# Sums of the MLP input's blocks kept in DRAM, and a second phase whose first operands are made in the first

## The chip, the cores and the metric

One core of one Trainium2 chip. The metric is the device time of one execution in microseconds; the output must agree with the reference.

## The reference, cut to what matters

One layer, 2048 tokens of width 1024, attention with a forget gate, then an MLP of width 4096. The change is in the MLP:

```python
x = x + g_m * fox_mixer(h, ...)                      # attention and its output projection
h = rms_norm(x, norm_mlp) * (1 + sc_f) + sh_f
x = x + g_f * (jnp.square(jax.nn.relu(h @ w_mlp_in)) @ w_mlp_out)
```

All of it is float32.

## The kernel before, in words

A float32 operand is held as two float32r parts: `split` makes the first by a cast on ACT (L754) and the second, the rest, by a subtraction on VectorE, DVE (L755). One product is then three matmuls (`mm3`, L139 to L141), first by first, first by rest, rest by first.

The two MLP products use a block scheme with seven products for eight (the Strassen-Winograd form). Operands are cut two by two, and products are named P1 to P7: P1 and P2 take blocks as they are, P6, P7, P5 and P4 take sums, P3 a sum on one side. The tokens are done in two halves s = 0, 1, each of two blocks of 512.

*Attention and output projection* come first; the projection works through 16 blocks of 128 tokens (`out_project`, 48 matmuls each). Beside it, from a list `side` of generators that are run one step at a time, the normed input h of the MLP is transposed (`turn`) and stored in DRAM as `h2_d`, for the first eight blocks; after the last of these, `prep_x(0)` loads the blocks B00 and B10 of h and splits them.

*Phase one* (h times W1, then relu and square) is a list of 224 slots, 112 for each half, one product of 12 matmuls in each. Jobs of kind X hold P1 and P2, jobs of kind Y hold P6, P7, P5, P4 and P3; each half begins with four X jobs, so that the first Y job is its ninth slot, and ends with four Y jobs. `prepare`, three slots ahead, blends the blocks of W1 on GpSimd (POOL, L966) and splits them. On the side, in a list `aux`, one generator step per slot: `prep_t(s)` loads four blocks of h for each of four kk, blends them on POOL into T1 to T4 (L807 to L814, 16 instructions a half) and splits five operands; then eight `turn_later` scale and transpose the tokens 1024 to 2047; then `prep_x(1)`, and after the last slot of the first half `prep_t(1)`. `mix` blends the results (four POOL instructions per Y job) for phase two, and `late` holds their stores to DRAM (`a_d`, `s_d`; L1058, for the last ones L1077), all on SP's queue.

*Phase two* (the result times W2) opens new SBUF pools on the memory of phase one's and runs 224 steps (s, product, p), 16 p to each of seven products, 12 matmuls a step, in the order P1, P2, P6, P7, P5, P4, P3. `fetch` (six steps ahead) loads, `blend` (five ahead) makes sums of W2's blocks on POOL, `divide` (four ahead) splits. B00, T1 = B01 - B00 and B11 stay in SBUF for both halves; P6, P7 and P4 blend from them through a ring `t` of four tiles. At the end of a product `collect` takes the four PSUM banks, and `emit` queues two POOL instructions for each output tile at once (L1160, L1161).

Pools are planned by the framework, which also sets the order of the instructions on each engine: what stands first in the text goes first where it can, and what is ready is let past. Each tile waits for the last use of what lay in its place.

## Time and profile before

| | us |
|---|---|
| median of 3 runs | 2987.9 (2984.85 to 2988.86) |
| profiled execution, its own time | 2984.72 |
| its span | 2983.0 |
| TensorE busy | 2677.2 (90%) |
| DVE busy | 2244.8 (75%) |
| ACT busy | 1654.7 (55%) |
| POOL busy | 1587.5 (53%) |

The span is the time from the first to the last instruction. Busy matmuls overlap, so a busy TensorE is not one at its pace. Phase one runs from about 1668 to 2325 us, phase two from 2340 to 2978. In the windows below a number with x is a count of instructions; PEclk is the clock granted to TensorE as a share of its full one; DMA is the mean busy share of 16 engines.

### The profile page before, as it was taken

What the parts mean: (1) busy time and instruction counts of PE and PEld (TensorE: products, weight loads), DVE (VectorE), ACT (ScalarE), POOL (GpSimd) and SP (SyncE); (2) the same over time, 40 slices, a digit from 0 to 9 for tenths busy, and PEclk for the clock granted to TensorE, in tenths of its full rate; (3) what the DMA queues carried; (4) which work ended last, traced back from release to release, by engine and by line L of the source; (5) the groups of instructions that cost most, each with busy time, mean ns of one, the idle gap of its engine ahead of it and who ended that gap; (6) DMA issues with size and microseconds to landing.
All of it is one profiled execution on the core that took longest, in us unless ns stands there. A gap on an engine that the chain in (4) does not pass through costs nothing. (4 is left out here: it accounts for less than half of the span.)

```text
span 2983.0 us, 46313 instructions
## 1 busy us (share of the span) xinstructions
PE 2677.2 (90%) x15819; PEld 2229.1 (75%) x15819; DVE 2244.8 (75%) x3695; ACT 1654.7 (55%) x2915; POOL 1587.5 (53%) x1143
## 2 busy tenths in 40 slices
PE   4789888888888898987899899998999899999998
PEld 4677777777777777776678678887888687788787
DVE  6689888888888887878733576678555589785977
ACT  4466666767676676766533366555555343344333
POOL 3344454646455454644622665578655457742955
PEclk9789899999999999998999999999999899999999
DMA  8479999999999998997956567766655863555344
GB/s 280 130 170 199 207 202 203 214 207 218 215 211 204 209 197 188 189 201 163 216 202 219 152 202 238 226 216 198 203 183 169 302 203 96 157 171 155 103 141 135
DMA packets 910445, 573.79 MB, mean 192 GB/s; under 512 B 595060, under 2 KB 775356, under 8 KB 910208
## 3 DMA queue, kind: packets, MB, share of 16 engines
q1 hardware_dynamic: 907024, 559.82, 74.6%
q0 software_dynamic: 3184, 11.01, 1.0%
q8 instruction: 124, 2.03, 0.3%
q14 instruction: 113, 0.93, 0.1%
HBM read 327.28 MB, written 100.80 MB: 144 GB/s over the span
## 5 line engine op out<-in xcount | busy, mean ns | idle before, releaser
L582 DVE SCALAR_TENSOR_TENSOR ph<-L,ph 128x1024 f16<-128x1024 f32 (+7 forms) x384 | 435.3, 1144 | 84.9 <-ACT ph L570 83.1
L415 POOL TENSOR_TENSOR hl<-hl,hh 128x1024 fp32r<-128x1024 f32 x120 | 298.7, 2491 | 253.0 <-ACT hh L414 218.8
L570 ACT ACTIVATE ph<-L 128x1024 f16<-128x1024 f32 (+7 forms) x384 | 301.8, 804 | 173.9 <-DMA pT<-ph 149.8
L495 PE MATMUL psq<-w,hh 128*128 128x384 f32 (+1 forms) x960 | 343.9, 359 | 26.0 <-DVE v L504 11.8
L139 PE MATMUL yP<-obP,oaP 128*128 128x512 f32 x896 | 344.3, 392 | 20.8 <-ACT obP L754 20.8
L140 PE MATMUL yP<-obP,oaP 128*128 128x512 f32 x896 | 353.0, 394 | 9.9 <-DVE obP L755 9.9
L497 PE MATMUL psq<-w,hl 128*128 128x384 f32 (+1 forms) x960 | 355.1, 372 | 6.7 <-POOL hl L415 6.6
L552 DVE CUSTOM_DVE_ANT_0 L<-S,F 128x1024 f32<-128x1024 f32 (+7 forms) x384 | 343.1, 904 | 23.1 <-PE S L546 8.5
L563 ACT ACTIVATE L<-L,st 128x128 f32<-128x128 f32 (+15 forms) x256 | 306.7, 1198 | 85.4 <-DVE st L557 81.3
L141 PE MATMUL yP<-obP,oaP 128*128 128x512 f32 x896 | 350.2, 391 | 0.0
L496 PE MATMUL psq<-w,hh 128*128 128x384 f32 (+1 forms) x960 | 342.6, 359 | 5.2 <-POOL w L341 5.2
L608 PE MATMUL po<-v,pT 128*128 128x128 f16 x2176 | 273.7, 227 | 58.8 <-DMA pT<-ph 50.3
L545 PE MATMUL S<-kT,qT 128*128 128x512 f32 (+3 forms) x640 | 259.4, 407 | 73.4 <-DVE mx L552 63.8
L755 DVE TENSOR_TENSOR oaP<-aP,oaP 128x512 fp32r<-128x512 f32 x224 | 244.5, 1092 | 97.8 <-ACT oaP L754 97.8
L754 ACT CAST oaP<-aP 128x512 fp32r<-128x512 f32 x224 | 139.3, 622 | 247.3 <-PE yP L141 232.3
L608 PEld LDWEIGHTS <-pT 128*128 128x128 f16 x2176 | 201.7, 102 | 90.6 <-DMA pT<-ph 63.9
L609 PE MATMUL po<-v,pT 128*128 128x64 f16 x2176 | 255.9, 199 | 0.0
L546 PE MATMUL S<-kT,qT 128*128 128x512 f32 (+3 forms) x640 | 238.2, 380 | 0.0
L609 PEld LDWEIGHTS <-pT 128*128 128x128 f16 x2176 | 195.5, 101 | 41.3 <-issue 30.4
L1127 POOL TENSOR_TENSOR tP<-B,B 128x512 f32<-128x512 f32 x96 | 155.7, 1626 | 115.0 <-DVE obP L755 114.9
L495 PEld LDWEIGHTS psq<-w,hh 128*128 128x128 f32 x960 | 191.3, 199 | 31.5 <-ACT hh L414 13.8
L139 PEld LDWEIGHTS yP<-obP,oaP 128*128 128x128 f32 x896 | 169.3, 189 | 57.4 <-ACT obP L754 22.1
(257 smaller groups left out, 7016.9 us busy)
## 6 DMA issues: line engine op xcount, KB each, us to landing
hl<-hT_d SPq DMA_DIRECT2D x120, 512.0 KB
w_Y_A<-in_w_mlp_in_dram SPq DMA_DIRECT2D x128, 256.0 KB
aP<-s_d SPq DMA_DIRECT2D x128, 256.0 KB
a_d<-c SPq DMA_DIRECT2D x96, 256.0 KB
aP<-a_d SPq DMA_DIRECT2D x96, 256.0 KB
F<-nF_d SPq DMA_DIRECT2D x64, 256.0 KB
wa<-in_w_ada_dram SPq DMA_DIRECT2D x32, 512.0 KB
w_X_A<-in_w_mlp_in_dram SPq DMA_DIRECT2D x64, 256.0 KB
```

Source lines behind the costliest of these rows:

```text
L139: nc.tensor.matmul(ps, lhsT=a[0], rhs=b[0], start=first, stop=False)
L140: nc.tensor.matmul(ps, lhsT=a[0], rhs=b[1], start=False, stop=False)
L141: nc.tensor.matmul(ps, lhsT=a[1], rhs=b[0], start=False, stop=last)
L495: nc.tensor.matmul(ps[:, :n], lhsT=hh, rhs=w[:, 0, :n], start=(kb == 0), stop=False)
L496: nc.tensor.matmul(ps[:, :n], lhsT=hh, rhs=w[:, 1, :n], start=False, stop=False)
L497: nc.tensor.matmul(ps[:, :n], lhsT=hl, rhs=w[:, 0, :n], start=False, stop=(kb == KB - 1))
L552: nc.vector.tensor_tensor_reduce(out=L[:, c0:c1], in0=s2[:, :c1 - c0], in1=Fb[g, h, cch // 2][:, :c1 - c0], scale=1.0, scalar=-3.0e38, op0 ...
L563: nc.scalar.activation(L[:, :W], L[:, :W], AF.Exp, bias=st[:, h:h + 1], scale=1.0, accum_out=st[:, 2 + h:3 + h])
L570: nc.scalar.activation(ph[:, :w], L[:, s0:s0 + w], AF.Copy, scale=PSCALE)
L582: nc.vector.scalar_tensor_tensor(ph[:, w:w + c], L[:, s0:s0 + c], PSCALE, ph[:, :c], op0=ALU.mult, op1=ALU.subtract)
L608: nc.tensor.matmul(po[:, h, :], lhsT=pT[:, bb, :], rhs=v, start=(b == 0), stop=False)
L609: nc.tensor.matmul(po[:, h, 0:HD], lhsT=pT[:, nw + bb, :], rhs=v[:, 0:HD], start=False, stop=(b == nb - 1))
```

## The change

The sums T1 to T4 of h are made by a new generator `mix_h`: in `side` for the first half, after the last `turn_later` for the second. They are stored to DRAM (`ht_d`), and `prep_t` loads them and B11 from there and only splits them, T4 and B11 with the cast on POOL in place of ACT. `prep_x` loads one generator step ahead of its split. `turn` has one step more between scaling and transposes for the later tokens. The operands of the first four steps of phase two are made in phase one (`early_ops`), in tiles that the X jobs leave free, and the 48 matmuls are issued before the pools are closed; the last late stores go on POOL's queue. In phase two T2 = B11 - B01 + B00 stays in SBUF in place of T1, so that P7, P5 and P4 need one blend each and P6 of the second half none. The two POOL instructions and the store of an output tile are spread over the steps of the next product (`emit_some`), one tile a step, and the small rings lie in a pool of their own, placed first.

```diff
@@ -80,6 +80,8 @@
     a_d = [[dram.tile([P, TJ], F32, name=f"a_d{j}_{fb}") for fb in range(NFB)] for j in range(NJ)]
     s_d = [[[dram.tile([P, TJ], F32, name=f"s_d{s}_{p}_{n}") for n in range(4)] for p in range(NFB // 2)]
            for s in range(NJ // 2)]
+    ht_d = {(s, k, n): dram.tile([P, TJ], F32, name=f"ht_d{s}_{k}_{n}") for s in range(NJ // 2)
+            for k in range(KB // 2) for n in ("T1", "T2", "T3", "T4")}
 
 
...
@@ -767,6 +769,8 @@
             xt = xh(hf)
             nc.vector.tensor_scalar(xt, xt, rs2[:, i:i + 1], None, op0=ALU.mult)
             yield
+            if i >= NA:
+                yield
             pt = psT.tile([P, TJ], F32, tag="T", name=f"xt2_{i}_{hf}")
             for k in range(KH):
                 nc.tensor.transpose(pt[:, blk[k]], xt[:, blk[k]], ident)
@@ -786,35 +790,65 @@
         nc.sync.dma_start(r.rearrange("p (t c) -> p t c", t=RB), h2_d[2 * s + t][:, k * KH + kk])
         return r
 
-    def keep(name, s, kk, raw):
+    def keep(name, s, kk, raw, pool=False):
         if name in ("B00", "B10"):
             w = hxp.tile([P, 2, TJ], F32R, tag="h", name=f"{name}_{s}_{kk}", bufs=2 * KH)
         else:
             w = sb.tile([P, 2, TJ], F32R, tag="hT", name=f"{name}_{s}_{kk}", bufs=5 * KH)
-        split(w, raw)
+        if pool:
+            nc.gpsimd.tensor_copy(w[:, 0, :], raw)
+            nc.vector.tensor_tensor(w[:, 1, :], raw, w[:, 0, :].bitcast(F32), op=ALU.subtract)
+        else:
+            split(w, raw)
         hop[name, s, kk] = (w[:, 0, :], w[:, 1, :])
 
     def prep_x(s):
         for kk in range(KH):
             for k in range(2):
-                keep(f"B{k}0", s, kk, load_h(s, k, 0, kk))
+                r = load_h(s, k, 0, kk)
                 yield
-
-    def prep_t(s):
+                keep(f"B{k}0", s, kk, r)
+
+    HT = ("T2", "T1", "T3", "T4")
+
+    def mix_h(s):
+
         for kk in range(KH):
             b00, b01, b11, b10 = [load_h(s, k, t, kk) for k, t in ((0, 0), (0, 1), (1, 1), (1, 0))]
+            yield
             t1, t2 = [ring("hs", [P, TJ], F32, f"ht{n}_{s}_{kk}") for n in range(2)]
             nc.gpsimd.tensor_tensor(t1, b01, b00, op=ALU.subtract)
             nc.gpsimd.tensor_tensor(t2, b11, t1, op=ALU.subtract)
-            keep("T2", s, kk, t2)
-            keep("T1", s, kk, t1)
             yield
             nc.gpsimd.tensor_tensor(b01, b11, b01, op=ALU.subtract)
-            keep("T3", s, kk, b01)
             nc.gpsimd.tensor_tensor(b10, b10, t2, op=ALU.subtract)
-            keep("T4", s, kk, b10)
-            keep("B11", s, kk, b11)
+            nc.sync.dma_start(ht_d[s, kk, "T2"], t2)
+            nc.sync.dma_start(ht_d[s, kk, "T1"], t1)
             yield
+            nc.sync.dma_start(ht_d[s, kk, "T3"], b01)
+            nc.sync.dma_start(ht_d[s, kk, "T4"], b10)
+
+    def prep_t(s):
+        def load(kk):
+            rs = []
+            for nm in HT:
+                r = ring("hs", [P, TJ], F32, f"hl{nm}_{s}_{kk}")
+                nc.sync.dma_start(r, ht_d[s, kk, nm])
+                rs.append(r)
+            return rs
+        nxt = load(0)
+        for kk in range(KH):
+            rs = nxt
+            keep("T2", s, kk, rs[0])
+            keep("T1", s, kk, rs[1])
+            yield
+            keep("T3", s, kk, rs[2])
+            keep("T4", s, kk, rs[3], pool=True)
+            b11 = load_h(s, 1, 1, kk)
+            if kk < KH - 1:
+                nxt = load(kk + 1)
+            yield
+            keep("B11", s, kk, b11, pool=True)
 
...
@@ -880,7 +914,7 @@
         if i < NA:
             soon.append(turn(i, held_x(xt)))
         if i == NA:
-            soon.append(prep_x(0))
+            soon += [mix_h(0), prep_x(0)]
...
@@ -1045,9 +1079,26 @@
         elif prod == "P3":
             finish(job, 0, 1, ps, got["165", s, p])
 
+    NE, ops = 4, {}
+
+    def early_ops():
+
+        for p in range(NE):
+            rs = [ring("hs", [P, TJ], F32, f"ea{p}"), ring("hs", [P, TJ], F32, f"eb{p}")]
+            nc.sync.dma_start(rs[0], a_d[0][p])
+            nc.sync.dma_start(rs[1], w2[p * P:(p + 1) * P, halves[0]])
+            yield
+            ops[0, "P1", p] = []
+            for r in rs:
+                w = hxp.tile([P, 2, TJ], F32R, tag="h", name=f"eo{p}", bufs=2 * KH)
+                split(w, r)
+                ops[0, "P1", p].append(w)
+            yield
+
     LOOK = 3
-    aux = [prep_t(0)] + [turn_later(i) for i in range(NA, NT)]
+    aux = [prep_t(0)] + [turn_later(i) for i in range(NA, NT)] + [mix_h(1)]
     n_last_x = max(n for n, (job, prod) in enumerate(slots) if job.s == 0 and job.kind == "X")
+    n_end_x = max(n for n, (job, prod) in enumerate(slots) if job.kind == "X")
     n_last_y = max(n for n, (job, prod) in enumerate(slots) if job.s == 0)
     load_jobs()
     for n in range(LOOK):
@@ -1065,16 +1116,27 @@
         run(aux)
         if n == n_last_x:
             aux.append(prep_x(1))
+        if n == n_end_x:
+            aux.append(early_ops())
         if n == n_last_y:
             while aux:
                 run(aux)
             aux.append(prep_t(1))
         if n == 2 * Q - 1:
-            while len(aux) > NT - NA:
+            while len(aux) > NT - NA + 1:
                 run(aux)
     mix(slots[-1][0])
     for _, d, c in late:
-        nc.sync.dma_start(d, c)
+        nc.gpsimd.dma_start(d, c)
+    while aux:
+        run(aux)
+    banks = {}
+    for p in range(NE):
+        a, b = ops.pop((0, "P1", p))
+        for tb in range(RB):
+            if p == 0:
+                banks[tb] = psS.tile([P, TJ], F32, tag="S", name=f"yP1_0_{tb}")
+            mm3(banks[tb], (a[:, 0, blk[tb]], a[:, 1, blk[tb]]), (b[:, 0, :], b[:, 1, :]), p == 0, False)
...
@@ -1083,16 +1145,17 @@
 
 
 
+    se = ctx.enter_context(tc.tile_pool(name="p6", bufs=2, reuse_waits="tile"))
     sa = ctx.enter_context(tc.tile_pool(name="p4", bufs=2, reuse_waits="tile"))
     sb = ctx.enter_context(tc.tile_pool(name="p5", bufs=2, reuse_waits="tile"))
-    RING = {"rw": 9, "op": 12, "R": 3 * FP, "t": 4, "e": RB, "v": RB, "y": 4, "x1": 2, "gf": 1}
+    RING = {"rw": 9, "op": 12, "R": 3 * FP, "t": 3, "e": RB, "v": RB, "y": 4, "x1": 2, "gf": 1}
 
     def ring(tag, shape, dt, nm):
-        return (sa if tag in ("rw", "op") else sb).tile(shape, dt, tag=tag, name=nm, bufs=RING[tag])
+        return (sa if tag in ("rw", "op") else sb if tag == "R" else se).tile(shape, dt, tag=tag, name=nm, bufs=RING[tag])
 
     PORDER = ("P1", "P2", "P6", "P7", "P5", "P4", "P3")
     steps = [(s, prod, p) for s in range(NS) for prod in PORDER for p in range(FP)]
-    R, raw_a, raw_b, ops = {}, {}, {}, {}
+    R, raw_a, raw_b = {}, {}, {}
 
...
@@ -1107,33 +1170,40 @@
 
     def fetch(st_):
         s, prod, p = st_
+        if (s, prod) == (0, "P1") and p < NE:
+            return
         raw_a[st_] = ring("rw", [P, TJ], F32, f"a{prod}_{s}_{p}")
         nc.sync.dma_start(raw_a[st_], a_of(*st_))
         if prod == "P1" and s == 0:
             R["B00", p] = load_b("R", f"B00_{p}", p, 0, 0)
         elif prod in ("P2", "P4"):
             raw_b[st_] = load_b("rw", f"B10_{prod}{s}_{p}", p, 1, 0)
-        elif prod == "P6" and s == 0:
-            R["T1", p] = load_b("R", f"B01_{p}", p, 0, 1)
+        if prod == "P2" and s == 0 and p < NE:
+            R["B00", p] = load_b("R", f"B00_{p}", p, 0, 0)
+        if prod == "P6" and s == 0:
+            R["T2", p] = load_b("R", f"B01_{p}", p, 0, 1)
             R["B11", p] = load_b("R", f"B11_{p}", p, 1, 1)
 
     def blend(st_):
+
         s, prod, p = st_
         tt = nc.gpsimd.tensor_tensor
         if prod == "P6" and s == 0:
-            tt(R["T1", p], R["T1", p], R["B00", p], op=ALU.subtract)
-        if prod in ("P6", "P7", "P4"):
+            tt(R["T2", p], R["B11", p], R["T2", p], op=ALU.subtract)
+            tt(R["T2", p], R["T2", p], R["B00", p], op=ALU.add)
+        elif prod in ("P7", "P5"):
             t = ring("t", [P, TJ], F32, f"t{prod}_{s}_{p}")
-            tt(t, R["B11", p], R["T1", p], op=ALU.subtract)
-            if prod == "P7":
-                tt(t, t, R["B00", p], op=ALU.subtract)
-            elif prod == "P4":
-                tt(t, raw_b[st_], t, op=ALU.subtract)
+            x, y = ("T2", "B00") if prod == "P7" else ("B11", "T2")
+            tt(t, R[x, p], R[y, p], op=ALU.subtract)
             raw_b[st_] = t
+        elif prod == "P4":
+            tt(raw_b[st_], raw_b[st_], R["T2", p], op=ALU.subtract)
 
     def divide(st_):
         s, prod, p = st_
-        b = R[{"P1": "B00", "P5": "T1", "P3": "B11"}[prod], p] if prod in ("P1", "P5", "P3") else raw_b.pop(st_)
+        if (s, prod) == (0, "P1") and p < NE:
+            return
+        b = R[{"P1": "B00", "P6": "T2", "P3": "B11"}[prod], p] if prod in ("P1", "P6", "P3") else raw_b.pop(st_)
         out_ = []
         for nm, raw in (("a", raw_a.pop(st_)), ("b", b)):
             w = ring("op", [P, 2, TJ], F32R, f"o{nm}{prod}_{s}_{p}")
@@ -1142,8 +1212,7 @@
         ops[st_] = out_
 
     gf = ring("gf", [P, D], F32, "gate_bc1")
-    nc.sync.dma_start(gf, gate_d[1:2, :].broadcast_to([P, D]))
-    E, V, banks = {}, {}, {}
+    E, V = {}, {}
 
...
@@ -1156,10 +1225,21 @@
         nc.sync.dma_start(out[i * P:(i + 1) * P, halves[n]], y)
 
     def emit(s, t, n, tb, y):
-        x1 = load_x1(s, t, n, tb)
-        nc.gpsimd.tensor_tensor(y, y, gf[:, halves[n]], op=ALU.mult)
-        nc.gpsimd.tensor_tensor(y, y, x1, op=ALU.add)
-        pend.append((s, t, n, tb, y))
+        pend.append([s, t, n, tb, y])
+
+    def emit_some(p):
+
+        if p < RB and len(pend) > p:
+            s, t, n, tb, _ = pend[p]
+            pend[p].append(load_x1(s, t, n, tb))
+        if 1 <= p <= RB and len(pend) >= p:
+            s, t, n, tb, y, x1 = pend[p - 1]
+            nc.gpsimd.tensor_tensor(y, y, gf[:, halves[n]], op=ALU.mult)
+            nc.gpsimd.tensor_tensor(y, y, x1, op=ALU.add)
+        if p == RB + 2:
+            for k, e in enumerate(pend):
+                store(*e[:5])
+            pend.clear()
 
...
@@ -1209,10 +1289,14 @@
     for n, st_ in enumerate(steps):
         s, prod, p = st_
         final = (s, prod) == (NS - 1, PORDER[-1])
-        if p in (2, 4):
-            for _ in range(2):
-                if pend:
-                    store(*pend.pop(0))
+        emit_some(p)
+        if n == FP // 2:
+            nc.sync.dma_start(gf, gate_d[1:2, :].broadcast_to([P, D]))
+        if n < NE:
+            ahead(n, LOAD, fetch)
+            ahead(n, BLEND, blend)
+            ahead(n, SPLIT, divide)
+            continue
         ahead(n, LOAD, fetch)
         ahead(n, BLEND, blend)
         ahead(n, SPLIT, divide)
```

## Rows read from the trace of the kernel before

**Rows 1.** Timeline of TensorE, end of phase one, start of phase two: start, duration.

```profile
2318.67 0.39 PE L140 MATMUL mP<-T,wP 128*128 128x512 f32 x1
...
2325.02 0.39 PE L141 MATMUL mP<-B,wP 128*128 128x512 f32 x1
2340.27 2.08 PE L139 MATMUL yP<-obP,oaP 128*128 128x512 f32 x4 [14.86 <-ACT obP L754]
...
2346.66 0.39 PE L140 MATMUL yP<-obP,oaP 128*128 128x512 f32 x1
```

**Rows 2.** Windows: busy (x count) of PE, PEld, DVE, ACT, POOL; PEclk; DMA share; GB/s.

```profile
1600.00:1640.00 40.00, 40.00 (x186) 32.53 (x185) 8.31 (x13) 3.23 (x6) 9.45 (x9) 1.00 0.59 187
1680.00:1720.00 40.00, 30.84 (x96) 19.04 (x95) 36.33 (x32) 21.03 (x41) 33.77 (x22) 0.84 0.66 201
1900.00:1940.00 40.00, 40.00 (x178) 33.14 (x177) 22.46 (x30) 20.71 (x34) 19.49 (x14) 1.00 0.61 194
2000.00:2040.00 40.00, 32.07 (x129) 25.37 (x128) 38.72 (x32) 21.13 (x38) 37.51 (x24) 0.87 0.66 206
2320.00:2360.00 40.00, 25.14 (x99) 20.23 (x98) 17.17 (x26) 17.49 (x29) 5.04 (x4) 0.79 0.79 278
2360.00:2400.00 40.00, 40.00 (x178) 33.10 (x178) 38.17 (x28) 19.17 (x34) 33.51 (x20) 1.00 1.00 360
2480.00:2520.00 40.00, 36.80 (x154) 27.89 (x153) 40.00 (x31) 15.17 (x27) 36.78 (x23) 1.00 0.30 85
2580.00:2620.00 40.00, 36.53 (x152) 27.74 (x152) 34.16 (x28) 14.96 (x27) 34.53 (x23) 1.00 0.54 167
2750.00:2790.00 40.00, 40.00 (x178) 33.15 (x177) 40.00 (x27) 16.01 (x28) 37.72 (x23) 1.00 0.45 138
2900.00:2940.00 40.00, 33.97 (x140) 26.95 (x139) 30.39 (x31) 15.73 (x29) 31.55 (x22) 0.91 0.57 174
```

**Rows 3.** TensorE's waits from 1730 to 1900: in total, times, longest.

```profile
PE xt L772 <- DVE x L768: 6.0, 5, 2.2
```

**Rows 4.** One group of L755's instructions: duration in ns, minimum, median, maximum.

```profile
L755 DVE TENSOR_TENSOR obP<-tP,obP x96: 676/1777/1785, 2418.0 to 2929.8; 128x512 fp32r<-128x512 f32 x96
```

**Rows 5.** The same of the blends on L1127.

```profile
L1127 POOL TENSOR_TENSOR tP<-B,B x96: 1254/1735/1834, 2364.1 to 2921.3; 128x512 f32<-128x512 f32 x96
```

**Rows 6.** Timeline of DVE, at the start of the second half.

```profile
2014.58 0.68 DVE L994 TENSOR_TENSOR c<-mP,u 128x512 f32<-128x512 f32 x1
```

**Rows 7.** Timeline of POOL, before the last loss of phase two.

```profile
2894.46 1.74 POOL L1227 TENSOR_TENSOR e<-e,gate_bc 128x512 f32<-128x512 f32 x1
2896.16 1.74 POOL L1160 TENSOR_TENSOR y<-y,gate_bc 128x512 f32<-128x512 f32 x1
```

**Rows 8.** The chain that ended last, at the seam.

```profile
2331.66 1.27 POOL c L1014
2332.95 0.32 SPq L1077
...
2333.80 5.09 DMA aP<-a_d
2338.91 0.62 ACT oaP L754
```

**Rows 9.** POOL's casts in the attention (L449), ns as above.

```profile
L449 POOL CAST qT<-qT x64: 604/609/1701, 104.4 to 1398.8; 64x512 fp32r<-64x512 f32 x64
```

**Rows 10.** Other blends of phase two by line (L1131 as L1129): busy, mean.

```profile
L1129 POOL TENSOR_TENSOR tP<-tP,B 128x512 f32<-128x512 f32 x32 | 51.8, 1619 | 2.5
...
L1124 POOL TENSOR_TENSOR B<-B,B 128x512 f32<-128x512 f32 x16 | 26.9, 1712 | 29.8 <-DMA B<-in_w_mlp_out_dram 29.8
```

**Rows 11.** Waits of SP's queue, whole span.

```profile
SPq L1111 <- DVE oaP L755: 291.0, 144, 4.5
```

**Rows 12.** TensorE's waits from 2330 to the end.

```profile
PE yP L139 <- ACT obP L754: 20.8, 3, 14.9
PE yP L140 <- DVE obP L755: 9.9, 23, 0.9
```

## The prediction

> **What bounds the kernel now.** I read the timeline of TensorE first, to learn its own pace in the two MLP phases, then the windows, to see where it falls behind that pace, then the waits, to see on whom. 29 matmuls stand between the starts at 2318.67 and 2325.02 us, 28 steps, so one is issued each 0.2268 us, whatever the 0.39 that its row shows (they are pipelined); a slot of 12 takes 2.72 us [rows 1]. A 40 us window at that pace counts x178 (2360:2400 and 2750:2790), so a window with fewer has lost (178 - x) x 0.2268 us to idling or to a lower clock [rows 2]:
>
> start of phase one (1680:1720), 82 matmuls, 18.6 us; its second half (2000:2040), 49, 11.1; the seam between the phases (2320:2360), 79, 17.9; and four places of phase two (2480 and its repeat at 2800, 2580, 2900), 24 + 24 + 26 + 38 = 112, 25.4. With 6.0 us in five waits of the transposes in `turn_later` for the scaling one line before [rows 3] this makes 79.0 us above the pace. Nothing can give more: at the pace TensorE is the bound, and the change takes no matmul away.
>
> Why it idles is read from DVE and POOL. In the windows with losses both are near full (36.33 and 33.77 of 40; 38.72 and 37.51; 40.00 and 36.78) [rows 2]. They hold each other up: the subtraction of `split` (two inputs in SBUF) takes 0.68 us at best and 1.78 in the median where its raw comes from POOL, a blend on POOL 1.25 at best and 1.74 in the median [rows 4, 5]. DVE's addition that reads a PSUM bank takes 0.68 in the middle of such a stretch [rows 6]. While both are at it, POOL instructions start 1.70 us apart [rows 7]. So a POOL blend beside DVE's subtractions costs DVE 1.70 - 0.68 = 1.02 us, and a step with two blends takes 3.40 us where TensorE wants 2.72.
>
> At the seam the chain names SP: the stores of the last job's blends wait for POOL, on the same queue the first loads of phase two stand behind them, the first goes at 2333.80, lands after 5.09, the first cast runs at 2338.91, the first matmul at 2340.27 [rows 1, 8].
>
> **Part by part.** *Start of phase one.* `prep_t(0)` loses its 16 blends on POOL: 16 x 1.02 = 16.3 us of DVE's time in a stretch where DVE's queue sets T. It adds eight casts on POOL (T4 and B11, from ACT). The nearest row is POOL's cast of 512 columns, 0.61 us in the median and 1.70 at most [rows 9]; bounds: nothing, if no subtraction meets it, and 1.02 each, if it holds DVE up like a blend. I take 0.61, 4.9 us (0 to 8.2), since it reads one tensor and not two. The Trainium skill (SBUF — State Buffer, Who interferes with whom) speaks against this part: a DVE instruction with two SBUF inputs and a GpSimd one that reads SBUF lock each other out for the whole instruction, while ACT waits for nobody, so by it every cast that meets a subtraction would cost in full, 8.2 us here and about 2928 in all. For blends the trace agrees, 1.78 us against 0.68; for casts only the 1.70 hints at it. Net 11.4 us (8.1 to 16.3) of the 18.6. Against it: 20 loads in place of 16, four more of 262 KB, 2.9 us at the 360 GB/s of 2360:2400 if the DMA were the bound there (share 0.66, so I take none). Left over: 7.2 us (2.3 to 13.4).
>
> *Second half, `prep_t(1)`.* The same edit, the same 11.4 (8.1 to 16.3), where 11.1 us are lost: left 0.5 (0 to 3).
>
> *Where the blends go.* `mix_h(0)` runs in the out-projection, 1600:1640 or a little later: POOL is busy 9.45 of 40 there and gets 16 x 1.25 = 20.0 (alone, [rows 5]); DMA has 0.59 x 40 = 23.6 and gets 32 transfers, 8.4 MB, 23.3 at 360 GB/s, 46.9 of 40. The spill goes into the three row blocks left, some 34 us ahead of phase one. Queued behind are SP's loads of x and o, issued one block (48 matmuls, 11 us) early, and POOL's residual additions. I take nothing (0 to 3). `mix_h(1)` runs once a slot after all of `turn_later`, by my count of slots at about 1900 to 1940. POOL is busy 19.49 there and gets 20.0 to 27.8 (16 x 1.74): 39.5 to 47.3 of 40; the DMA 0.61 x 40 + 23.3 = 47.7 of 40. So both may be overfull by 7 or 8 us [rows 2]. What waits behind is POOL's blending of W1 for the next Y job, prepared three slots (8.2 us) early, of which two blends, a cast and a subtraction use about 2 x 1.25 + 0.6 + 0.7 to 1.8, 4 to 5 us. That leaves 3 to 4 us of cover: if one of the two overruns in full, 4 us are exposed; if both in turn, 11. I take 2 (0 to 11). `prep_t` reads all of it back: 72 more transfers on SP in all, 18.9 MB.
>
> *`turn`.* One more slot between scaling and transposes, 2.72 us, where the longest wait was 2.2 [rows 3]: 6.0 falls to 1 (0 to 4).
>
> *Seam.* Four steps, 48 matmuls or 10.9 us, have their operands ready before the phase ends, so the fifth is wanted at 2325.25 + 10.9 = 2336.1. The eight loads and eight splits for them run beside the last four Y jobs, in POOL's and DVE's light stretch (5.04 and 17.17 of 40 in 2320:2360, most of it after the seam). The late stores go to POOL's queue, where nothing follows for 20 us. With SP free the first loads need only their buffers; by my reading of the pools those of the fifth step lie on tiles used last at 2317 to 2325, so 2325 + 5.1 + 1.4 = 2331.5, in time. Left 0. If the first load still went at 2333.80, it would be 2340.3 - 2336.1 = 4.2 late, and with a slow restart 6.9: the sixteen matmuls from 2340.27 to 2346.66 took 6.4 us where the pace gives 3.6, at a granted clock of 0.79 over that window [rows 1, 2]. So 0 to 6.9.
>
> *Phase two.* The blends fall from 176 (96 + 32 + 32 + 16) [rows 5, 10] to 128. At P7 and P4 one is left per step: DVE needs one locked and one free subtraction, 1.70 + 0.68 = 2.38, under 2.72. P5 gets one, the same. P6 of the first half keeps two, but into its own tile, so they need no ring and can run in P1 and P2, 87 us in which POOL already does 16 of them; 32 x 1.70 = 54 fit. The eight output instructions, which stood ahead of blends in one row [rows 7], come two a step. The worst place is P4 of the second half: 16 blends, 8 outputs and 8 for the last stage, 32 x 1.70 = 54 us against 43.5 plus the six steps that the 12 operand tiles let it run ahead, 16: it fits by 5. Before it was 48, and 8.6 were lost. 2750:2790 shows that load with x178: 23 POOL instructions, DVE 40.00 of 40 [rows 2]. Left 2 of 25.4 (0 to 8).
>
> **Sum.** Left over: 7.2 + 0.5 + 0 + 2 + 1 + 0 + 2 = 12.7. Gain 79.0 - 12.7 = 66.3 us. The profiled execution took 2984.7 (span 2983.0), the median is 2987.9; with the same 3 us between them the forecast is 2987.9 - 66.3 = 2921.6, 2922. All bounds at their best: 79.0 - 2.3 = 76.7, 2911; all at their worst, 13.4 + 3 + 3 + 11 + 4 + 6.9 + 8 = 49.3 left, 2958.
>
> **Rivals.** *The stall only moves to 1900:1940*: the moved blends and the DMA overrun there one after the other. For it: both sums reach 47 of 40. Against: W1 is prepared early, and 2360:2400, with a DMA share of 1.00 and POOL at 33.51, loses nothing [rows 2]. 9 us more than forecast, 2931, and with the start bound by its 20 loads 2937.
>
> *The seam stays*: SBUF tiles come free too late. For: all of phase two lies on phase one's memory. Against: the reading of the pools above. 7 us, 2929; with a second wait of 3 us while the buffers refill, 2932.
>
> *POOL stays the bound in phase two*, since blends go on meeting outputs: half of 25.4 stays, 2922 + 10.7 = 2933.
>
> *Slower than before*: SP becomes the bound. `mix_h`'s 32 stores wait on SP for POOL, and behind them stand W1's loads and the stores that free result tiles. It takes 66.3 / 32 = 2.1 us exposed on TensorE per store to cancel the gain. For it: SP's waits for a result are about that long, 291.0 us in 144 waits, 2.0 each [rows 11]. At 2.5 each, 80 us, it is 2922 + 80 = 3002. Against: all these waits stand in phase two, where TensorE's waits come to 30.7 us in all [rows 12], half of it the seam: SP's waiting is mostly covered.
>
> *The change doesn't do it*: the order that is built differs from the written one and the early operands still wait. Then only phase two's relief comes, 25.4 - 2 = 23.4 us: 2964.
>
> **Chances.** Forecast, within its own 2911 to 2930, 0.60; stall moved 0.13; seam 0.08; phase two 0.10; not done 0.05; slower 0.04. Two of ten left out at both ends: the range goes from 2907 (the best case, less the 3 to 4 us by which runs differ) to 2946, which holds the three rivals and their pairs. A change of 0.2%, 6 us, can be told from none. Faster 0.94, same 0.02, slower 0.04.
>
> **What would show it.** In the profile after: start of phase one with about 7 us lost and no blends of h among POOL's instructions there; 2000:2040's counterpart near x178; a window at about 1900 that holds 16 more POOL instructions and, if I am wrong, fewer than x170; no wait above 1 us between the phases; phase two's windows at x178 and DVE below 38 of 40 in P7 and P4. I am wrong if TensorE gets waits for DMA that it does not have now, or if DVE stays full at the start of phase one because the casts lock it.

## The result, and the profile after

The changed kernel takes 2950.2 us in the median (2948.6 to 2951.1, four runs) beside 2987.4 of the kernel before: ratio 0.9865, interval [0.985, 0.988]. It is faster by 37.2 us; the forecast was 66.3, and 2950.2 lies above the range (2907 to 2946).

Windows of TensorE in the profile after, with the columns of [rows 2]:

```profile
1680.00:1720.00 40.00, 36.94 (x160) 29.30 (x159) 38.68 (x49) 25.51 (x50) 26.01 (x21) 1.00 0.87 281
1900.00:1940.00 40.00, 38.69 (x174) 31.72 (x173) 22.83 (x31) 23.75 (x44) 24.93 (x18) 1.00 0.82 272
1940.00:1980.00 40.00, 37.42 (x158) 30.27 (x157) 28.69 (x30) 17.68 (x32) 37.35 (x25) 0.96 1.00 344
2000.00:2040.00 40.00, 29.78 (x108) 22.83 (x107) 31.64 (x36) 16.22 (x30) 25.16 (x21) 0.83 0.87 274
2320.00:2360.00 40.00, 40.00 (x178) 33.12 (x177) 24.66 (x32) 20.68 (x34) 8.13 (x9) 1.00 0.83 296
2380.00:2420.00 40.00, 34.12 (x141) 25.26 (x140) 32.15 (x22) 17.40 (x29) 37.89 (x24) 1.00 0.74 243
2480.00:2520.00 40.00, 40.00 (x178) 33.11 (x178) 22.44 (x34) 16.76 (x30) 19.31 (x15) 1.00 0.34 98
2580.00:2620.00 40.00, 40.00 (x178) 33.14 (x177) 31.63 (x37) 17.79 (x32) 15.36 (x10) 1.00 0.61 193
2900.00:2940.00 40.00, 40.00 (x178) 33.11 (x178) 28.56 (x30) 12.57 (x22) 18.53 (x12) 1.00 0.31 96
```

Full pace is x178. The start of phase one went from x96 to x160, the seam (2320:2360) from x99 to x178, and the places of phase two are all at x178, with POOL at 15 to 19 of 40 where it had 31 to 37. But 2000:2040 fell from x129 to x108, 1940:1980 is short for the first time (x178 before), and 2380:2420 loses inside phase two's P2 (x178 before).

At the seam there is no gap left (timeline of TensorE after):

```profile
2325.23 0.39 PE L143 MATMUL mP<-B,wP 128*128 128x512 f32 x1
2325.46 0.39 PE L141 MATMUL yP<-eo,eo 128*128 128x512 f32 x1
```

For all further comparisons I added up, over the timeline of TensorE, the time from each start to the next less 0.2268 us per matmul (0.1 per transpose), by place: start (to 52 us after the first matmul of phase one), turn (to 235; the transposes of `turn_later`), mid (to 327; `mix_h(1)` and `prep_x(1)`), second half (to 385; `prep_t(1)`), P2 (up to 135 us into phase two, P1, P2 and P6, without the seam's wait and slow restart, 17.8 before). "Total" is over both phases, the seam and the rest of phase two with it. By this measure the kernel before loses 83.7 us and the one after 46.3: 37.4 less, close to the 37.2 between the medians. Phase one begins between 1664 and 1677 us in the profiles; e13, without the first half's round trip, begins at 1675 and the kernel before at 1668, so no relation to the edits is seen, and losses are safer to compare than times.

| kernel | median us, ratio to before [interval] | start | turn | mid + second | P2 | total |
|---|---|---|---|---|---|---|
| before | 2987.4 | 19.8 | 10.0 | 0 + 11.1 | 0 | 83.7 |
| after | 2950.2, 0.9865 [0.985, 0.988] | 5.6 | 10.5 | 6.3 + 15.9 | 8.6 | 46.3 |
| e1_no_mix1 | 2936.1, 0.9828 [0.981, 0.984] | 5.6 | 9.7 | 0 + 11.4 | 4.0 | 30.3 |
| e2_cast_act | 2945.2, 0.9859 [0.984, 0.988] | 3.6 | 7.9 | 4.4 + 15.8 | 7.1 | 38.4 |
| e3_swap | 2947.1, 0.9864 [0.985, 0.988] | 5.0 | 11.1 | 5.7 + 16.1 | 2.9 (seam 3.2) | 43.6 |
| e4_turn_old | 2940.8, 0.9853 [0.984, 0.987] | 6.1 | 14.5 | 0 + 13.0 | 4.3 | 37.5 |
| e5_q5 | 2944.1, 0.9868 [0.984, 0.990] | 6.4 | 9.4 | 3.6 + 13.0 | 7.1 | 39.2 |
| e6_less_split | 2938.6, 0.9848 [0.982, 0.987] | 5.6 | 8.7 | 5.2 + 9.4 | 3.8 | 32.2 |
| e7_turn_load | 2950.8, 0.9884 [0.986, 0.991] | 5.1 | 12.5 | 6.6 + 15.3 | 7.2 | 45.9 |
| e8_late_act | 2941.7, 0.9858 [0.983, 0.988] | 5.6 | 10.4 | 5.6 + 14.7 | 7.1 | 42.9 |
| e9_one_load | 2951.5, 0.9871 [0.985, 0.989] | 6.1 | 9.7 | 4.9 + 15.8 | 8.6 | 44.4 |
| e10_q6_spread | 2943.8, 0.9853 [0.983, 0.988] | 5.2 | 7.8 | 11.2 + 9.6 | 4.7 | 38.1 |
| e12_xload_act | 2941.8, 0.9845 [0.982, 0.987] | 6.1 | 7.0 | 2.4 + 15.5 | 7.3 | 38.0 |
| e13_no_mix0 | 2960.8, 0.9902 [0.988, 0.992] | 19.8 | 5.9 | 7.4 + 16.0 | 6.8 | 55.5 |
| e14_q5_later | 2945.1, 0.9849 [0.983, 0.987] | 6.4 | 9.5 | 2.3 + 12.4 | 7.1 | 37.3 |
| e15_combo | 2931.0, 0.9808 [0.979, 0.983] | 6.1 | 7.0 | 0 + 11.4 | 4.2 | 28.2 |
| e16_last_direct | 2946.9, 0.9868 [0.984, 0.989] | 5.1 | 12.6 | 6.4 + 14.6 | 3.2 | 41.4 |
| e17_combo2 | 2929.7, 0.9804 [0.979, 0.982] | 6.4 | 1.2 | 7.3 + 5.4 | 6.2 | 26.0 |
| e18_behind | 2940.1, 0.9838 [0.982, 0.986] | 6.4 | 9.8 | 2.0 + 13.1 | 7.2 | 38.0 |
| e19_combo3 | 2925.0, 0.9790 [0.977, 0.981] | 5.0 | 1.4 | 2.4 + 6.3 | 7.0 | 21.4 |

(In e17 the second half's first wait falls at 1995, into "mid"; only the sum of the two is to be read there.) e6, e9 and e16 leave a part of the computation out. Medians of the kernel before lie between 2985.6 and 2988.6, and executions of one kernel up to 17 us apart (e14), so the times of neighbours in the table don't tell them apart. The losses come from one profile each. Their scatter can be read from the runs whose edit lies behind a place: start 5.0 to 6.1, turn 8.7 to 12.6, mid 4.9 to 6.4, second half 14.6 to 16.1. What lies inside these bounds can't be told from no effect.

### The profile page after: what moved, and what is told of

Its sections match the earlier page's. It is cut to its first block, busy times and chain, and to the rows that moved or that the text cites. A ratio compares the mean times of both kernels' runs of the same rounds, so it can differ in the third digit from the quotient of the medians.

```text
span 2948.0 us, 46378 instructions
## 1 busy us (share of the span) xinstructions
PE 2664.8 (90%) x15819; PEld 2231.8 (76%) x15819; DVE 2150.5 (73%) x3695; ACT 1646.8 (56%) x2899; POOL 1509.0 (51%) x1116
## 5 line engine op out<-in xcount | busy, mean ns | idle before, releaser
L142 PE MATMUL yP<-obP,oaP 128*128 128x512 f32 x880 | 343.3, 390 | 3.9 <-DVE obP L757 3.9
L143 PE MATMUL yP<-obP,oaP 128*128 128x512 f32 x880 | 342.5, 389 | 0.0
L141 PE MATMUL yP<-obP,oaP 128*128 128x512 f32 x880 | 338.1, 389 | 2.0 <-ACT obP L756 2.0
L757 DVE TENSOR_TENSOR oaP<-aP,oaP 128x512 fp32r<-128x512 f32 x220 | 219.6, 998 | 143.9 <-ACT oaP L756 143.7
L141 PE MATMUL mP<-T,wP 128*128 128x512 f32 x512 | 201.4, 394 | 4.7 <-DVE u L1053 2.6
L142 PE MATMUL mP<-T,wP 128*128 128x512 f32 x512 | 200.7, 392 | 0.0
```

The lines of the kernel that those rows point to most:

```text
L141: nc.tensor.matmul(ps, lhsT=a[0], rhs=b[0], start=first, stop=False)
L142: nc.tensor.matmul(ps, lhsT=a[0], rhs=b[1], start=False, stop=False)
L143: nc.tensor.matmul(ps, lhsT=a[1], rhs=b[0], start=False, stop=last)
```

## Experiments

**Was it the blends of h that held the start up?**

```diff
- soon += [mix_h(0), prep_x(0)]      # and prep_t(0) in aux
+ soon += [prep_x(0)]                # and the old prep_t(0)
```

> The sums of the first half are made in phase one again, as in the kernel before, by 16 instructions on GpSimd; all the rest as in the changed kernel. The step of the prediction that held (these instructions held the vector engine up at the start of phase one) gives: the loss at the start goes back from 5.6 to 16 to 20 us, the time to 2960 to 2964. Rival (another edit emptied the start): the loss stays under 8 us and the time at 2950.

The loss at the start is back at 19.8 us, that of the kernel before. So taking the sixteen blends away was worth 14.2 us there, net of the reloads and casts that came for them. A part is given back: e13 loses 5.9 in the turn, the changed kernel 10.5. The casts cost little (POOL after, 1675 to 1725 us: busy, mean):

```profile
L799 POOL CAST B<-hr 128x512 fp32r<-128x512 f32 x4 | 4.2, 1052 | 0.0
L799 POOL CAST T<-hlT 128x512 fp32r<-128x512 f32 x4 | 3.9, 981 | 1.5 <-DMA hlT<-ht_d_T 1.5
```

**The casts put back on ACT.**

```diff
- if pool:
+ if False:
```

> The changed kernel with the casts of T4 and B11 on ACT again, not on POOL. Theory B (locks): eight casts fewer on POOL in each half free 8 x 1.02 = 8 us of DVE's time, so the start of the second half loses 9 in place of 17 us and the start of phase one 1 to 2 in place of 5: about 2940. Theory A: the data comes no earlier, 0 to 3 us: 2947 to 2950. If ACT's order is what matters, eight casts more on ACT ahead of its PSUM copies make it 1 to 4 us slower.

The start falls from 5.6 to 3.6, the second half stays at 15.8. At the start the eight casts cost some 2.0 us, not 8.2; the theory that they are what fills DVE in the second half fell. A cast does hold a subtraction up, but for less time than a blend does (DVE and POOL after, the first subtraction alone, the second beside the cast):

```profile
1696.32 0.68 DVE L757 TENSOR_TENSOR T<-hlT,T 128x512 fp32r<-128x512 f32 x1
...
1698.11 1.07 POOL L799 CAST T<-hlT 128x512 fp32r<-128x512 f32 x1
1698.63 1.09 DVE L757 TENSOR_TENSOR T<-hlT,T 128x512 fp32r<-128x512 f32 x1
```

That is 0.41 us for a cast where a blend costs 1.02 to 1.10. At the start seven of the eight casts meet a subtraction, 2.9 us of DVE's time.

**The second half without the round trip through DRAM.**

```diff
- ... for i in range(NA, NT)] + [mix_h(1)]     # and prep_t(1)
+ ... for i in range(NA, NT)]                  # and the old prep_t(1)
```

> The changed kernel, but the second half's sums T1 to T4 are made as before: no mix_h(1), and prep_t(1) loads four blocks, blends on POOL and splits, casts on ACT. Theory A (the round trip through DRAM overfills DMA and POOL at 1920 to 1985 us, share 1.00, and its late data is what makes the queues of ACT and DVE stand still at 2010 to 2031): the 6 us lost at 1935 to 1980 go, the 17 us at the start of the second half fall back to the 11 of the kernel before, 12 us faster, about 2938. Theory B (the second half's loss comes from DVE being full with splits beside POOL, wherever the sums come from): 16 blends come back for eight casts, the start of the second half loses 20 us or more, and the whole is 0 to 6 us slower, 2950 to 2956.

14 us faster than the changed kernel: 6.3 gone from mid, 4.5 from the second half, 4.6 from P2. In the second half the old way loses 11.4 (as in e15), what it lost before. So `mix_h(1)` only costs, some 11 us; P2's part goes with another wait (below), and e19, also without the round trip, loses 7.0 there. The same stretch in both, first after, then without the round trip (DMA share in the last column but one):

```profile
1920.00:1960.00 40.00, 38.69 (x171) 31.74 (x170) 20.86 (x24) 18.13 (x31) 37.46 (x26) 1.00 1.01 339
```

```profile
1920.00:1960.00 40.00, 40.00 (x178) 33.11 (x177) 28.89 (x34) 24.05 (x42) 29.86 (x20) 1.00 0.75 244
```

**The extra step in `turn` taken out**, which also brings the round trip 44 us forward.

```diff
- if i >= NA:
-     yield
```

> The changed kernel without the added generator step between scaling and transposes of the later tokens, so that turn_later ends sixteen slots (44 us) earlier and mix_h(1) runs at about 1880 to 1940 and not beside prep_x(1). Theory C (the scaling is late because its data and the chain of small DVE instructions behind POOL's locks are late, a slot more or less does not matter): the waits of the transposes stay at 5 to 8 us, and the second half gains from the earlier round trip, 5 to 12 us: 2938 to 2945. Rival (the step does what it is for): 6 to 10 us more of such waits, 2956 to 2960.

The turn gets worse, 14.5 for 10.5: the extra step gives some 4.0 us. Mid falls to 0. The round trip now runs from 1875 to 1916 us, and TensorE loses nothing beside it, though the DMA and POOL are as full as in the changed kernel (window of e4, POOL last but three):

```profile
1880.00:1920.00 40.00, 40.00 (x178) 33.10 (x178) 24.37 (x26) 17.62 (x31) 39.84 (x28) 1.00 1.00 347
```

So full DMA and POOL do not cost by themselves. What is different in the changed kernel is that `prep_x(1)` runs at the same time. Of the 6.3 us in mid, 1.6 are lost around 1937, where ACT's cast waits for POOL's blend of W1, and the other 4.7 from 1973 on, where TensorE waits 2.6 us for DVE's `u`, and `u` stands behind splits of `prep_x(1)` (DVE after):

```profile
1971.78 3.45 DVE L757 TENSOR_TENSOR B<-hr,B 128x512 fp32r<-128x512 f32 x2
1975.15 0.68 DVE L1053 TENSOR_TENSOR u<-mP,u 128x512 f32<-128x512 f32 x1
```

**SBUF pools of phase two exchanged**, so that the resident blocks of W2 lie elsewhere.

```diff
- sa = ...(name="p4"); sb = ...(name="p5")
+ sb = ...(name="p5"); sa = ...(name="p4")
```

> The changed kernel with two SBUF pools of phase two in the other order: the W2 blocks that stay (R) lie ahead of the rings for raws and operands, so that the first sixteen of them no longer lie on the result tiles whose last stores land at 2340 us. Theory: the 8.5 us lost at 2390 to 2418 are the 9.0 us in which SP stood behind such a store while the DMA was idle, given back fifty us later by a DMA that is full from 2340 to 2400. Then they go: 7 to 9 us faster, about 2942. Rival: P2's loads and the R blocks together are more than the DMA can move in time in any case (28 MB from 2323 to 2412 us is 315 GB/s), and POOL's two blends per step lock DVE: 0 to 3 us.

P2 falls to 2.9, but 3.2 come back at the seam: another buffer waits now, an operand of a cast, for a late store of the same kind (ACT of e3):

```profile
2343.71 0.62 ACT L756 CAST obP<-B 128x512 fp32r<-128x512 f32 x1 [12.10 <-DMA s_d<-c]
```

**Who makes P2 late?** After, SP stands 9.0 us behind a store, in its timeline and then in its waits:

```profile
2330.96 0.32 SPq L1176 DMA_DIRECT2D aP<-a_d  x1
2340.31 0.33 SPq L1168 DMA_DIRECT2D B<-in_w_mlp_out_dram  x1
```

```profile
SPq L1168 <- DMA s_d<-c: 9.0, 1, 9.0
```

By that wait the load fills memory that the last late store still reads; POOL issues the store at 2335.01, behind its sums (timeline of POOL):

```profile
2333.22 1.31 POOL L1048 TENSOR_TENSOR c<-c,s 128x512 f32<-128x512 f32 x1
2334.46 0.56 POOL L1130 DMA_DIRECT2D s_d<-a  x1
2335.01 0.54 POOL L1130 DMA_DIRECT2D s_d<-c  x1
```

```diff
- nc.gpsimd.dma_start(d, c)
+ nc.scalar.dma_start(d, c)
```

> The last late stores of phase one are issued by the scalar engine instead of GpSimd. Theory (the stand of SyncE behind the last store makes the loads of phase two's second step late): the wait for that store falls from 9.0 to about 4 us, the loss in P1, P2 and P6 from 8.6 to about 4, and the time is about 2946. Rival (full DMA queues alone set that loss): the wait falls and the loss stays 8 us or more, the time 2949 to 2951.

Neither came out: SP now stands behind three late stores (3.7, 3.5 and 1.9 us, 9.1 in all), and the loss is 7.1. The last stand ends 11.1 us after phase two's first matmul, where it ended after 14.9, but it is as long in all. Then the sums ahead of the stores; they are left out and the results stored as they are:

```diff
- mix(slots[-1][0])
+ late.extend((now[0] + 2, d, c) for d, c in zip(s_d[...], (got["c", 1, 0], ...)))
```

> The last job's four sums for phase two are left out and its results stored as they are, so a part of the computation is missing and the output is not the reference's. Theory (SyncE stands behind the last late store, which waits for those sums on GpSimd): the stand falls from 9.0 to 2 to 4 us and the loss in P1, P2 and P6 from 8.6 to 3 to 4.5. Rival (the amount of data in that stretch sets the loss): the stand falls and the loss stays at 7 us or more.

No such wait is left, and P2 loses 3.2. In the sixteen profiles with one such stand, loss and stand go together: stands of 2.7 to 5.3 us lose 3.8 to 4.7 (e10, e15, e6, e1, e4), stands of 5.9 to 9.0 lose 6.2 to 8.6. Which late store SP stands behind differs between them, also where the edit lies far off (one of `s`, 4.6 us, in e1; of `a`, 6.5, in e2; of `c`, 9.0, after); why was not followed up. The loads that SP puts off run at a DMA share of 1.05 in 2350:2390 (after), so nothing is caught up.

**The turn: x loaded earlier.**

```diff
- if i >= NA:            # in turn
-     yield
+ yield                  # in turn_later, between load and square
+ yield
```

> In the turn from the first half to the second the loads of x are issued two steps further ahead of the square that reads them, with the number of slots of the kernel before. Theory (the loads of x land late): the scalar engine's waits for x fall from 19.7 us to under 5, the loss at the turn from 10.5 to 1 to 3 us, and the time is about 2942. Rival (the chain of small vector-engine operations behind the square, held up by GpSimd's locks): the waits for x fall, the loss at the turn stays 6 to 10 us, the time 2946 to 2950.

No better: 12.5, and ACT's waits for x are 26.7 us. SP issues the first loads no earlier (30.6 us after phase one's first matmul, 30.5 in the changed kernel). The wait that costs most, after (L133, 1.25 us from 1739.40, stands just ahead of these lines):

```profile
1740.68 1.18 DVE L134 TENSOR_TENSOR t_x<-t_x,v_x 128x1 f32<-128x1 f32 x1
...
1742.09 1.00 DVE L136 TENSOR_TENSOR y_x<-y_x,t_x 128x1 f32<-128x1 f32 x1
...
1743.31 1.77 DVE L770 TENSOR_SCALAR x<-x,rs 128x512 f32<-128x512 f32 x2
1744.74 1.12 PE L776 MATMUL xt<-ident,x 128*128 128x128 f32 x4 [3.95 <-DVE x L770]
```

```diff
- nc.sync.dma_start(xt, x1_d[i][:, halves[hf]])
+ nc.scalar.dma_start(xt, x1_d[i][:, halves[hf]])
```

> The loads of x in the turn are issued by the scalar engine, so they do not stand on SyncE's queue behind stores and weight loads that wait for GpSimd. Theory (SyncE's queue delays them by some 4 us): the longest wait of the transposes, 4.1 us at 1740 us, falls under 1.5, with it goes the slow restart of 12 matmuls behind it, 2.4 us; the loss at the turn falls from 10.5 to 3 to 5 us. Rival (the chain of small vector-engine operations under GpSimd's lock): the wait stays above 3 us and the loss above 8.

ACT's waits for x fall from 19.1 to 7.1 us and the turn from 10.5 to 7.0, but the longest wait of the transposes stays at 3.1 (3.9 after): SP's queue is one part, the chain behind the square (after: load at 1729.54, square at 1734.28, scaling at 1743.31) the other. The waits for x are no measure of the loss by themselves: they are 21.2 us in e13, which loses 5.9, and 6.1 in e4, which loses 14.5.

**The second half.** After, TensorE waits for ACT's copy of a PSUM bank there (waits of TensorE, 1900 to 2060; the 2.6 and one of 1.3 are those of mid):

```profile
PE mP L141 <- ACT p L1065: 9.5, 2, 5.3
PE mP L141 <- DVE u L1053: 2.6, 1, 2.6
PE mP L141 <- ACT wP L756: 2.1, 2, 1.3
```

The kernel before waited there for the same copy, and not for what it waited for at the start of phase one (waits of TensorE before, 1675 to 1725, then 1990 to 2060):

```profile
PE mP L140 <- DVE T L755: 6.6, 8, 2.2
```

```profile
PE mP L139 <- ACT p L1031: 7.9, 2, 7.3
```

After, that copy stands on ACT behind the relu of the last Y job, and the relu waits for DVE's sum (`c`, 2007.91), ahead of which DVE runs eight splits from 1998.32 on. Some of DVE's queue, and of ACT's:

```profile
2002.21 1.09 DVE L757 TENSOR_TENSOR T<-hlT,T 128x512 fp32r<-128x512 f32 x1
2003.23 0.68 DVE L1053 TENSOR_TENSOR u<-mP,u 128x512 f32<-128x512 f32 x1
2003.83 1.75 DVE L757 TENSOR_TENSOR T<-hlT,T 128x512 fp32r<-128x512 f32 x1
2005.51 0.68 DVE L757 TENSOR_TENSOR wP<-w_X_A,wP 128x512 fp32r<-128x512 f32 x1
...
2007.91 0.68 DVE L1028 TENSOR_TENSOR c<-mP,u 128x512 f32<-128x512 f32 x1
```

```profile
2005.33 0.62 ACT L756 CAST T<-hlT 128x512 fp32r<-128x512 f32 x1 [1.90 <-DMA hlT<-ht_d_T]
2008.67 0.63 ACT L1029 ACTIVATE c<-c 128x512 f32<-128x512 f32 x1 [2.73 <-DVE c L1028]
...
2015.13 0.57 ACT L1065 COPY p<-mP 128x512 f32<-128x512 f32 x1
```

Three causes offer themselves: too many splits, their order, late data. Fewer splits:

```diff
- split(w, raw)
+ copy_split(w, raw)     # two copies on ACT, for T3, T4, B11 of s = 1
```

> The operands T3, T4 and B11 of the second half get a copy by the scalar engine in place of the vector engine's subtraction for their second part, so a part of the split is left out and the output is not the reference's. Theory (too much vector-engine work in the second half): the loss in that half falls from 15.9 to 6 us or less and the time to about 2940. Rival (late data): the loss stays at 12 us or more, the time at 2946 or more.

15.9 fell to 9.4, between the theories: the amount counts for some 6.5. (The edit also takes POOL's casts of T4 and B11 there away, which e2 shows to cost nothing in this half.) Data there in time:

```diff
- nxt = load(kk + 1)
+ nxt = load(kk + 1) if s == 0 else rs
```

> In the second half the sums T1 to T4 are loaded for the first kk only and used for all four, so twelve loads are left out and the products are not the reference's; the vector engine's work is the same. Theory (too much vector-engine work in too few slots): the loss in the second half stays at 13 us or more. Rival (the reloaded sums land late and hold up the scalar engine's in-order queue): it falls from 15.9 to about 8 us or less. With both at work it lies between, and the rest of the sum is what the run with fewer subtractions gave, 6.5 us.

15.8: late data alone explain nothing. DVE is full (window of e9):

```profile
2000.00:2020.00 20.00, 13.62 (x54) 10.86 (x53) 20.00 (x20) 10.01 (x19) 16.34 (x13) 0.83 0.40 131
```

More time for the same work:

```diff
- Q = 4
+ Q = 5
```

> Five X jobs instead of four stand ahead of the first Y job in each half, so the vector engine has more matmul time in which to make the operands of the half's first Y jobs. Theory (more vector-engine work than its place holds): the loss in the second half falls from 15.9 to about 9 us, that at the start of phase one from 5.6 to 1 to 3, and the time from 2950 to about 2940 us. Rival (the data land late, or an order on a queue is at fault): both losses stay within 2 us and the time is 2948 to 2952.

Neither theory: mid and second half fall from 22.2 to 16.6, the start not at all.

```diff
- Q = 4                 # prep_t: two steps for a kk
+ Q = 6                 # prep_t: three steps for a kk
```

> Six X jobs ahead of the first Y job in each half, and the splits of a half's operands spread over twelve slots instead of eight, so that the vector engine has 32.7 us of matmul time for the same work instead of 21.8. Theory (too much vector-engine work in too few slots): the losses at the start of phase one and in the second half fall from 5.6 and 15.9 us to 1 to 4 each, and the time is 2933 to 2938. Rival (late data or the order on a queue): the second half stays at 12 us or more, the time at 2944 or more.

The second half falls to 9.6, but `mix_h(1)` now runs later and mid loses 11.2. Together 20.8: given back.

```diff
- if n == n_last_y: ...; aux.append(prep_t(1))
+ if n == n_last_y + 2: aux.append(prep_t(1))        # Q = 5
```

> Five X jobs ahead of the first Y job, and the splits of the second half begin two slots later, so they don't stand on the vector engine's queue ahead of the last sums of the first half, which free the PSUM banks; their number and the slots they have are about those of the changed kernel. Theory (the order: the reloaded operands are all ready at once, and ten splits go ahead of those sums): the loss in the second half falls from 15.9 (13.0 with five X jobs alone) to 7 or less. Rival (the amount of the vector engine's work alone): it stays at 11 to 14 us.

12.4, but this run decides nothing: the first split runs at 1995.51 (1995.65 in e5, 1996.15 after), since the framework lets ready work past what is written ahead of it. So the order was forced:

```diff
+ with tc.issue_after(last_sum), tc.issue_after(last_square):
      keep(...)         # the second half's T and B11; Q = 5
```

> Five X jobs ahead of the first Y job, and an explicit edge that issues the second half's splits on the vector engine, and their casts on the scalar engine, behind the last sum and the last square of the first half; beside the run with five X jobs alone only the order differs. Theory (the order: eleven splits go ahead of the three sums that free the PSUM banks): the wait of some 7 us at 2008 goes, and the loss from the middle to the end of the second half's start falls from 16.6 to 9 us or less. Rival (the amount): the wait moves to the first Y job, and 13 us or more stay.

15.1 of 16.6 stay. DVE now does the sums in time, and the next thing in line is late: ACT's copy stands behind casts that wait for reloaded sums (timeline of ACT, e18):

```profile
2010.04 0.62 ACT L756 CAST T<-hlT 128x512 fp32r<-128x512 f32 x1 [2.18 <-DMA hlT<-ht_d_T]
2011.73 0.62 ACT L756 CAST T<-hlT 128x512 fp32r<-128x512 f32 x1 [1.08 <-DMA hlT<-ht_d_T]
2013.44 0.62 ACT L756 CAST T<-hlT 128x512 fp32r<-128x512 f32 x1 [1.08 <-DMA hlT<-ht_d_T]
2013.96 0.58 ACT L1076 COPY p<-mP 128x512 f32<-128x512 f32 x1
```

So neither order nor data alone is the bound; each hides behind the other. Both at once were not tried with the round trip kept.

**Combinations** of edits shown above:

```diff
+ the old prep_t(1), no mix_h(1); x on nc.scalar's queue     # e15, e17, e19
+ Q = 5, prep_t(1) appended two slots later                  # e17
+ Q = 6, issue_after for the second half's splits            # e19
```

> Two edits at once: the sums of the second half are made in phase one as in the kernel before, and x is loaded on the scalar engine's queue in the turn. If the losses are separate, those of the changed kernel fall by what each run gave: mid from 6.3 to 0, the turn from 10.5 to about 7, the second half to 11.4, P2 to about 4, in all to about 27 us of the 46.3, and the time is about 2931. Rival (both gained at the same place): the sum stays at 30 or more, the time at 2936.

> The edits of the combination with five X jobs ahead of the first Y job, and the second half's operands begun two slots later. If the order on the vector engine's queue counts here too, the loss in the second half falls from 11.4 to 6 or less and the time to 2925 to 2929; if not, it is that of the combination, about 2931.

> The combination without the second half's round trip and with x on the scalar engine's queue, six X jobs ahead of the first Y job, and the same explicit edge. Theory (order, with slots enough for the amount): the loss there falls from 12.7 (with five X jobs and no edge) to 6 or less, and the time from 2929.7 to 2921 to 2925. Rival (amount, or the lock by GpSimd's blends): 11 us or more stay, the time is 2928 or more.

The parts add up: e15 loses 28.2, as expected 27. In e17 the turn falls to 1.2, which neither Q = 5 (9.4) nor x on ACT (7.0) did alone; why was not followed up. Its second half stays at 12.7 (mid included); with Q = 6 and the order it is 8.7, between that run's theory (6 or less) and its rival (11 or more). e19 takes 2925.0 us, ratio 0.979 [0.977, 0.981], and beats both kernels. What it still loses in the second half is waits for DVE's `c` (6.0 us in three).

## Why the prediction was wrong, step by step

*Start of phase one*: right. Forecast 7.2 left, 5.6 measured; before, TensorE waited there for the splits of T themselves, and e13 shows the blends as the cause. The casts were priced too high, 4.9 for some 2.0. The Trainium skill (SBUF — State Buffer, Who interferes with whom) has a GpSimd instruction that reads SBUF lock out a DVE instruction with two SBUF inputs; the trace agrees for casts too, 1.09 us for 0.68. The 8.2 in the prediction took the hold of a blend, 1.02, for that of a cast, which is 0.41.

*Seam and the four places of phase two*: right. 17.9 and 25.4 us went to 0, as their windows show. No run takes the edits behind them out one at a time, so which of them did it (fewer blends or outputs spread out in phase two, early operands or the stores' queue at the seam) is not shown.

*"Second half, the same edit, the same 11.4 ..., left 0.5"*: this step failed, and it is the largest: 15.9 left, 15.4 us of the miss. A saving was carried from one place to another because the code was the same, but the waits were not: at the start TensorE waited for splits of T (6.6 us), in the second half for ACT's copy of a PSUM bank (7.9), and the prediction did not read which. That copy stands at the end of a chain of in-order queues, splits ahead of the last Y jobs' sums on DVE, casts ahead of the copy on ACT, and POOL has those jobs' sums to do as well (eight of L1045 to L1048 between 1997 and 2039). Without the round trip 11.4 are lost there (e1), with it 15.9: nothing is gained and 4.5 are added. How the 15.9 divide between the amount of splitting (some 6.5, by e6), its order and late data stays open.

*"One more slot ... 6.0 falls to 1"*: failed; 10.5, 9.5 of the miss. The wait was placed between scaling and transposes. The slot gives some 4.0 (e4), but the wait begins further back: x is issued late on SP's queue (some 3.5 us, by e12), and the small DVE operations behind the square take up to 1.25 us each. And the first half's round trip costs the turn some 4.5, a term that the prediction doesn't have: with the extra step 5.9 are lost without it (e13) and 10.5 with it, without the step 10.0 (before) and 14.5 (e4). What carries this over was not followed up. The term was also read too small: TensorE's waits were 6.0, the loss by the pace 10.0. A part of the difference is slow matmuls, at a granted clock of 0.75 in 1787:1792, behind a wait of 2.1 us (before).

*`mix_h(1)`, "2 (0 to 11)"*: 6.3, inside its bounds. The DMA and POOL filled as forecast, and the wait that was foreseen, behind POOL's blends of W1, came, but it costs 1.6 us. The other 4.7 are lost behind the splits of `prep_x(1)` on DVE, which the prediction doesn't count. The first rival, with a chance of 0.13, named the place; its cause, DMA and POOL overrunning, costs nothing in e4.

*Phase two, "left 2"*: the places named lose nothing, but P2 loses 8.6, 6.6 more. The step behind it is the seam's "The late stores go to POOL's queue, where nothing follows for 20 us", with its reading of the pools for the fifth step alone. That is true for the fifth step, not for the loads behind it: one of them fills a tile that the last store still reads, and the whole of SP's queue stands for it (e16).

Together: 15.4 + 9.5 + 4.3 + 6.6 - 1.6 (start) = 34.2 us more left than the 12.7 forecast, 46.9; measured are 46.3. The gain is short by 29.1 only, since the kernel before lost 83.7 us and not 79.0. The 46.3 lie just under the sum of all the worst bounds (49.3), but that is luck: the second half (0 to 3), the turn (0 to 4) and P2 (phase two, 0 to 8) are outside their own.

## What to carry to other kernels

A saving estimated at one place is not a price for the same code at another: read which wait ends last at each, what else stands on those queues there, and which of it comes next once the first wait is gone. What moved work costs depends on what runs beside it, and full engines alone don't tell: the same round trip cost 6.3 us beside the splits of `prep_x(1)` and nothing in the stretch 44 us earlier, with the DMA at a share of about 1.00 both times. A buffer whose last reader is a store makes the next load's whole queue wait, here 9.0 us with the stores on POOL's queue and 9.1 on ACT's.

## Not expected of the hardware

Operations of DVE on 128x1 that read two tensors in SBUF take 1.00 to 1.25 us beside POOL's blends and 0.15 alone (L946 at 1737.42, while POOL stands still): they lose 0.85 to 1.1 us, nearly as much as one on 128x512 does by a blend, 1.1 [rows 4]. The three of the chain at 1739.40 take 3.4 us together; for its x ACT had waited 1.05.

After the 3.95 us wait at 1740 the twelve matmuls from 1745.51 take 5.21 us in place of 2.72; the granted clock of that stretch is 0.50, the lower of the two levels (1.2 of 2.4 GHz):

```profile
1745.00:1750.00 5.00, 5.00 (x15) 4.04 (x15) 4.39 (x7) 3.65 (x8) 1.29 (x1) 0.50 0.28 106
1751.00:1754.00 3.00, 3.00 (x15) 2.49 (x14) 2.21 (x3) 1.74 (x4) 2.12 (x2) 1.00 1.09 333
```

So the wait costs 3.95 + 2.49 = 6.4 us.
